# A two-layer hybrid encoder in split fp32: activation sums in program order, squares on VectorE, adding DMAs pinned

## The chip, the cores and the metric

The kernel runs on one core of a Trainium2 chip. Its time is the device time of one execution in microseconds (us); three executions gave 2105.25 (median), 2104.72 and 2109.62. The engines are named as in the profile: PE is TensorE, DVE is VectorE, ACT is ScalarE, POOL is GpSimd, SP is SyncE. Each engine takes its instructions in order; semaphores tie the engines together.

## The reference, cut to what matters

The program is a stack of two layers on x of 512 tokens by 1024 features. `D_FF` is 2816, that is 22 tiles of 128.

```python
def rms_norm(x, g):
    y = x * lax.rsqrt(jnp.mean(x * x, axis=-1, keepdims=True) + EPS)
    return y * g
def swiglu(u, w_gate, w_up, w_down):
    return (jax.nn.silu(u @ w_gate) * (u @ w_up)) @ w_down
...
for i in range(DEPTH):
    x = x + 0.5 * swiglu(rms_norm(x, ffn1_norm[i]), ffn1_w_gate[i], ffn1_w_up[i], ffn1_w_down[i])
    z = rms_norm(x, mix_norm[i]) @ w_in[i]
    ...   # four mixers on column groups of z: y_na, y_swa, y_dil, y_mla
    y = jnp.concatenate([rms_norm(y_na, ...), rms_norm(y_swa, ...), rms_norm(y_dil, ...), rms_norm(y_mla, ...)], axis=-1)
    x = x + y @ w_out[i]
    x = x + 0.5 * swiglu(rms_norm(x, ffn2_norm[i]), ffn2_w_gate[i], ffn2_w_up[i], ffn2_w_down[i])
    gate = jax.nn.sigmoid(rms_norm(x, ple_norm[i]) @ ple_w_gate[i])
    x = x + gate * (p[i] @ ple_w_proj[i])
return rms_norm(x, final_norm)
```

## The kernel before

**Numbers.** Everything is float32, but PE multiplies in fp32r. Each operand is therefore split into a high part (a rounding copy on ACT) and a low part (the difference, on DVE), and a product is three matmuls: wh with x high, wh with x low, wl with x high (`mm3`, lines 303 to 305). `cut` (L236 on ACT, L237 on DVE) splits a weight piece into a tile wh and a tile wl, three of each. `feed` with `split` (L156 on ACT, L157 on DVE) splits one 128 x 512 tile x[m] of the activations, times its norm gain. x is held transposed, features on partitions, as eight tiles x[0] to x[7].

**Norms.** The division by the root mean square comes after the matmul. For it, each x[m] is squared (L318 on ACT) and added to `acc` (L319: on POOL for m = 1 to 6, on DVE for m = 7). `rstat` sums over partitions on PE (L330), scales on DVE (L333) and takes the power -0.5 on POOL (L334, tile rc). `rspread` spreads rc over the partitions by PE transposes (L341) and copies the result to rb on ACT (L348); the gate of a tile waits for rb.

**The feed-forward.** An FFN goes over 22 tiles f in two halves of 12 and 10. Each f needs a gate matrix and an up matrix product. The first two f are "direct": four pieces each, every piece 12 matmuls on 512 columns. From there f goes in pairs. The gate stays dense (four "d" pieces of 12 matmuls by 512 columns a pair), but the up matrices of the pair and the two halves of the tokens make a 2 x 2 block product, done by seven products instead of eight (`seven`; a "product" is 12 matmuls of 256 columns, L412). ORDER interleaves them, `"ssdssdssdsd"`, and S_STEPS names the seven: X1, Z1, X2, Y, X3, Z2, X4. These need sums of activations (`combos`, L383 to L394, tiles TC, four sets a norm, made once per FFN) and sums of weight blocks (tiles S, four buffers). After the first half, and again after the second, the down projection runs eight output tiles.

**Sums of weights.** They are made by DMA: SP loads one block into S (L254), then POOL issues a DMA that adds another block from DRAM onto it (L256). For the next pair `sums` makes s1 = a21 + a22 and s2 = a21 + a22 + a11, so s2 takes two adding DMAs, here called s2a and s2b, and s2b must wait until s2a has landed. `factors` makes s3 = a11 + a21, and adds a12 onto s2 (L271, here "the a12 add") once s2 has been cut for its first use. The sum s2 + a12 is then cut again; it is the weight of the product Z2, the sixth of the pair.

**What sets the order.** The generator `plan` gives the weight pieces in the order of use; `take` pops one and `prep` keeps two ahead in the FFN. SP and PE run in the order written. On DVE, ACT and POOL a scheduler chooses the order, except for instructions handed to `keep_in_program_order` (also through `hold`, while `held` is true: at the start of the program).

**Crossings.** A stage hands x to the next one by adding its output to x[m], splitting x[m], squaring it. This document calls the end of the mixer's output projection (L1004 adds to x[m]) with the start of the second FFN "mixer to FFN 2", and the end of layer 0 (`ple_out`) with the start of layer 1 "gate to FFN 1". Mixer to FFN 2 occurs once in each layer, gate to FFN 1 once.

Of the kernel before, what the change touches and what calls it, by code (L numbers as in the profile page):

```python
# [18 lines left out]
KC = 8  # L19
# [18 lines left out]
class Encoder:  # L38
# [121 lines left out]
    def plan(self):  # L160
        a = self.a
        full = ((0, 4, 128), (512, 4, 128))
        for l in range(self.depth):
            for w in range(2):
                gu = a["ffn_gu"][l, w]
                for half in range(2):
                    c0, c1 = CUT[half], CUT[half + 1]
                    for f in range(c0, c1, 2):
                        if f == 0:
                            for n, g in enumerate(self.direct(l == w == 0, gu)):  # L170
                                yield g
                                if n == (4 if l == w == 0 else 7):
                                    sums = self.sums(gu[2, 1], gu[3, 1])
                            continue
                        s = self.factors(gu[f, 1], gu[f + 1, 1], sums)
                        d = self.slices((gu[f, 0], full), (gu[f + 1, 0], full))
                        for n, c in enumerate(ORDER):
                            yield s if c == "s" else d
                            if n == 3 and f + 2 < FF:
                                sums = self.sums(gu[f + 2, 1], gu[f + 3, 1])  # L180
                    for m in range(KC):
                        dn = a["ffn_d"][l, w, m]
                        yield from self.each((dn[:, c0:c0 + 8], full), (dn[:, c0 + 8:c1], ((0, c1 - c0 - 8, 128),)))
                if w == 0:
                    for i in range(M_END):
                        if i == M_DQ0:
                            for j in range(2):
                                yield from self.each((a["w_up"][l, j], ((0, 2, 256), (512, 1, 256))))
                        yield from self.each((a["w_in"][l, i], full))
                    for i in range(8):  # L190
                        yield from self.each((a["w_out"][l, i], full))
            for m in range(KC):
                pl = a["ple"][l, m]
                yield from self.each((pl[:, 0:4], ((0, 4, 128),)), (pl[:, 4:10], ((0, 3, 128), (384, 3, 128))))

    def direct(self, opening, gu):
        full = ((0, 4, 128), (512, 4, 128))
# [48 lines left out]
    def sums(self, a, b):  # L246

        flat = lambda src, k: src[:, k:k + 4].rearrange("p k m -> p (k m)")
        a11, a12, a21, a22 = flat(a, 0), flat(a, 4), flat(b, 0), flat(b, 4)
        nc = self.nc  # L250

        def load(first, *more):
            t = self.own("S", [128, T], F32, 4)
            nc.sync.dma_start(t, first)  # L254
            for src in more:
                nc.gpsimd.dma_start(t, src, accum_op=ALU.add)  # L256
            return t

        s1 = load(a21, a22)
        s2 = load(a21, a22, a11)  # L260
        return s1, s2, lambda: load(a11, a21), a12

    def factors(self, a, b, sums):
        s1, s2, third, a12 = sums
        raw, half = self.load(a), self.raw()
        yield self.cut(raw[:, 0:512], 4)
        s3 = third()
        yield self.cut(s1, 4)
        self.nc.sync.dma_start(half[:, 0:512], b[:, 4:8].rearrange("p k m -> p (k m)"))
        yield self.cut(s2, 4)  # L270
        self.nc.gpsimd.dma_start(s2, a12, accum_op=ALU.add)  # L271
        yield self.cut(raw[:, 512:1024], 4)
        yield self.cut(s3, 4)
        yield self.cut(s2, 4)
        yield self.cut(half[:, 0:512], 4)
# [48 lines left out]
    def rstat(self, acc, n, more=None):  # L324
        nc = self.nc
        ss = self.small()
        parts = [acc] if more is None else [acc, more]
        for i, p in enumerate(parts):
            for t in range(4):
                nc.tensor.matmul(ss[:, t:t + 1], lhsT=p[:, t * 128:(t + 1) * 128], rhs=self.ones,  # L330
                                 start=i == t == 0, stop=i == len(parts) - 1 and t == 3, skip_group_check=True)
        rc = self.tile("rc", [128, 4], F32, 3)
        nc.vector.tensor_scalar(out=rc, in0=ss[:, 0:4], scalar1=1.0 / n, scalar2=EPS, op0=ALU.mult, op1=ALU.add)  # L333
        nc.gpsimd.tensor_tensor(out=rc, in0=rc, in1=self.nhalf, op=ALU.pow)  # L334
        return rc

    def spread(self, rc):
# [13 lines left out]
    def begin(self, l, off):  # L351
        self.norm = (l, off)
        self.nacc = self.acc()
        self.xn = []

    def feed(self, m, square=True):
        nc = self.nc
        l, off = self.norm
        t = self.act()
        if l < self.depth:  # L360
            self.split(t, self.x[m], self.g(l, off, m))
        else:
            if m < KC - 1:
                self.squared(m)
            else:
                self.last = self.tmp()
                nc.scalar.activation(self.last, self.x[m], AF.Square)
            square = False
            t = t[:, 0].bitcast(F32)
            nc.scalar.activation(t, self.x[m], AF.Copy, scale=self.g(l, 0, m))  # L370
        self.xn.append(t)
        if square:
            self.squared(m)

    def squared(self, m, eng=None):
        nc = self.nc
        self.square(self.nacc, self.x[m], m == 0, eng or (nc.vector if m == KC - 1 else nc.gpsimd))

    def combos(self, l, off, j):
        nc = self.nc  # L380
        xg = self.keep().bitcast(F32)
        for e in range(2):
            nc.scalar.activation(xg[:, e], self.x[2 * j + e], AF.Copy, scale=self.g(l, off, 2 * j + e))  # L383
        f = self.keep().bitcast(F32).rearrange("p e (h t) -> p (e h) t", h=2)
        q = xg.rearrange("p e (h t) -> p (e h) t", h=2)
        nc.vector.tensor_tensor(out=f[:, 0:2], in0=q[:, 0::3], in1=q[:, 1:2].to_broadcast([128, 2, HT]),
                                op=ALU.subtract)
        nc.vector.scalar_tensor_tensor(f[:, 2], f[:, 0], -1.0, q[:, 3], op0=ALU.mult, op1=ALU.subtract)
        nc.vector.scalar_tensor_tensor(f[:, 3], f[:, 2], -1.0, q[:, 2], op0=ALU.mult, op1=ALU.subtract)
        out = []  # L390
        for i in (0, 2):
            t = self.own("TC", [128, 2, T], F32R, 8).rearrange("p e (h t) -> p e h t", h=2)
            nc.scalar.activation(t[:, :, 0], f[:, i:i + 2], AF.Copy)
            nc.vector.tensor_tensor(out=t[:, :, 1], in0=f[:, i:i + 2], in1=t[:, :, 0].bitcast(F32), op=ALU.subtract)  # L394
            out.append(t)
        return out

    def right(self, name, xs, tn):
        out = []
# [57 lines left out]
    def opening(self, gp, up):  # L457
# [5 lines left out]
                self.mm3(ps, (w[0][:, k % 4:], w[1][:, k % 4:]), xs[k:k + 1], start=k == 0, stop=k == KC - 1)  # L463
        for m in range(KC):
            self.squared(m, self.nc.vector)
        self.held = False

    def ffn(self, l, w, nxt):
        nc, a = self.nc, self.a
        xs, acc, rb, rc = self.xn, self.nacc, None, None  # L470
        off = G_FFN2 if w else G_FFN1
        self.ahead = 2
        tn, held = [], []
        for half in range(2):
            nf = CUT[half + 1] - CUT[half]
            hs = [self.big() if f < 7 else self.keep() for f in range(nf)]
            for f in range(2 if half == 0 else 0):
                gp, up = self.dense(), self.small()
                if l == w == f == 0:
                    self.opening(gp, up)  # L480
# [3 lines left out]
                if rc is not None:  # L484
                    rb, rc = self.rspread(rc), None
                    for j, hj in enumerate(held):
                        self.gated(*hj, rb, hs[j])
                    held = []
                self.mm3(gp, self.take(), xs[4:], start=False)
                self.full(up, xs)  # L490
                if rb is None:
                    rc = self.rstat(acc, D)
                    held.append((gp, up))
                else:
                    self.gated(gp, up, rb, hs[f])
            if half == 0:
                tn = [self.combos(l, off, j) for j in range(4)]
            for f in range(0 if half else 2, nf, 2):
                u = self.keep().bitcast(F32)
                s = self.seven(xs, tn, u)  # L500
                gps, grs, nd = [None] * 2, [None] * 2, 0
                for c in ORDER:
                    if c == "d":
                        e, part = divmod(nd, 2)
                        nd += 1
                        if part == 0:
                            gps[e] = self.dense()
                            self.mm3(gps[e], self.take(), xs[0:4], stop=False)
                            continue
                        self.mm3(gps[e], self.take(), xs[4:8], start=False)  # L510
                        grs[e] = self.gate(gps[e], rb)
# [387 lines left out]
    def mix(self, l, nxt):  # L899
# [103 lines left out]
        def out(m):  # L1003
            nc.vector.tensor_tensor(self.x[m], self.x[m], self.ops[m], op=ALU.add)  # L1004
            self.feed(m)

        for m in range(4):
            if m % 2 == 0:
# [68 lines left out]
    def ple_out(self, m, gp, pp, rb):  # L1077
# [4 lines left out]
        nc.vector.scalar_tensor_tensor(gr, gr, 1.0, pp, op0=ALU.add, op1=ALU.mult)  # L1082
        nc.vector.scalar_tensor_tensor(self.x[m], gr, 0.5, self.x[m], op0=ALU.mult, op1=ALU.add)
        self.feed(m)

    def ple_in(self, l):
        nc, a = self.nc, self.a
# [178 lines left out]
```

## Time and profile before

| | |
|---|---|
| median of three runs (lowest, highest) | 2105.25 us (2104.72, 2109.62) |
| profiled execution | 2106.33 us, its span 2104.6 us |
| PE | busy 2061.2 us, 98% of the span |
| DVE, ACT, POOL | 65%, 52%, 19% |
| granted TensorE clock, mean | 0.996 |
| chain that ended last, by engine | PE 88%, DVE 5%, ACT 3%, DMA 1%, issue 1% |

The span runs from the first to the last instruction; the profiled execution's own time is 1.7 us longer. Times inside the span are counted from its start. An arrow, as in `ps<-act,wl`, reads output from inputs. `[0.87 <-DVE wl L237]` after a row means that the engine sat idle 0.87 us before it and that DVE's instruction of line 237 on tile wl ended that wait. A row of a DMA issued by POOL has the time that POOL spent on the issue; the data land later.

### The profile page before, as it was taken

Reading aid. Unit: us, or ns where it says so; the run is one execution under the profiler, and the core shown is the slowest. Engines: PE = TensorE matmul, PEld = TensorE weight load, DVE = VectorE, ACT = ScalarE, POOL = GpSimd, SP = SyncE. Lnnn points to the kernel's source line nnn. Section 1 sums busy time; section 2 is a strip of 40 time slices with the busy share of each in tenths; the row PEclk is TensorE's granted clock in tenths of the full one; section 3 lists DMA queues with packets and bytes.
Section 4 is the critical chain, followed back from the end, with each engine's and each line's share of the span. In section 5 each row is a group of like instructions: output and inputs, shape, how many; then the busy total and the mean of one; then the engine's idle time right before and its main releaser. Section 6 shows DMA issues by size and latency. Waiting matters only on the chain.

```text
span 2104.6 us, 30073 instructions
## 1 busy us (share of the span) xinstructions
PE 2061.2 (98%) x11028; PEld 1761.4 (84%) x11028; DVE 1365.0 (65%) x2282; ACT 1089.1 (52%) x2057; POOL 393.5 (19%) x391
## 2 busy tenths in 40 slices
PE   8999999999999999999999999999999999999998
PEld 6988988887877988988889889888878789889886
DVE  7654666777777654666766546667787766546655
ACT  6442444687865442444644324437777644334434
POOL 2200101043322200101121002011433321002011
PEclk9999999999999999999999999999999999999999
DMA  7764753323126754753367457433121267457432
GB/s 221 181 163 115 189 135 112 96 66 81 51 61 150 188 145 118 187 140 103 118 148 191 131 137 177 125 102 108 62 81 60 67 167 183 125 144 182 128 93 85
DMA packets 109604, 269.07 MB, mean 128 GB/s; under 512 B 12688, under 2 KB 16912, under 8 KB 109456
## 3 DMA queue, kind: packets, MB, share of 16 engines
q1 hardware_dynamic: 79232, 208.89, 31.3%
q0 software_dynamic: 30080, 58.21, 16.2%
q8 instruction: 86, 1.41, 0.3%
q14 instruction: 62, 0.51, 0.1%
q10 hardware_dynamic: 144, 0.05, 0.0%
HBM read 262.91 MB, written 2.10 MB: 126 GB/s over the span
## 4 chain that ended last, share of the span: by engine, by line
PE 88%; DVE 5%; ACT 3%; DMA 1%; issue 1%; POOL 0%; SPq 0%; DVEq 0%; ACTq 0%; POOLq 0%
PE s L412 16%; PE ps L304 15%; PE ps L303 15%; PE ps L305 15%; PE s L303 6%; PE s L304 6%; PE s L305 6%; PE ps L412 3%; PE pv L677 2%; PE s L661 2%; ACT tmp L547 1%; PE s L619 1%; PE s L620 1%; DVE PT L665 1%; PE s L330 1%
## 5 line engine op out<-in xcount | busy, mean ns | idle before, releaser
L236 ACT ACTIVATE wh<-raw 128x512 fp32r<-128x512 f32 (+2 forms) x668 | 408.2, 612 | 578.9 <-PE ps L304 254.9
L237 DVE TENSOR_TENSOR wl<-raw,wh 128x512 fp32r<-128x512 f32 (+2 forms) x594 | 415.4, 700 | 259.3 <-ACT wh L236 251.6
L256 POOL DMA_DIRECT2D S<-in_ffn_gu x160 | 139.5, 880 | 910.1 <-DMA S<-in_ffn_gu 536.1
L303 PE MATMUL ps<-big,wh 128*128 128x512 f32 x632 | 253.0, 400 | 0.4 <-ACT big L156 0.4
L305 PE MATMUL ps<-big,wl 128*128 128x512 f32 x632 | 247.8, 392 | 3.1 <-DVE wl L237 3.1
L304 PE MATMUL ps<-big,wh 128*128 128x512 f32 x632 | 248.1, 393 | 0.9 <-DVE big L157 0.9
L303 PE MATMUL ps<-act,wh 128*128 128x512 f32 x624 | 248.9, 399 | 0.0
L305 PE MATMUL ps<-act,wl 128*128 128x512 f32 x624 | 244.2, 391 | 3.1 <-DVE wl L237 3.1
L304 PE MATMUL ps<-act,wh 128*128 128x512 f32 x624 | 244.4, 392 | 0.6 <-DVE act L157 0.6
L412 PE MATMUL s<-TC,wh 128*128 128x256 f32 x1280 | 236.1, 282 | 0.7 <-ACT rb L348 0.7
L412 PEld LDWEIGHTS s<-TC,wh 128*128 128x128 f32 x1280 | 205.7, 189 | 10.3 <-ACT rb L348 0.9
L237 DVE TENSOR_TENSOR wl<-S,wh 128x512 fp32r<-128x512 f32 x160 | 110.8, 692 | 122.3 <-ACT wh L236 121.1
L412 PE MATMUL s<-TC,wl 128*128 128x256 f32 x640 | 181.4, 283 | 0.0
L236 ACT ACTIVATE wh<-S 128x512 fp32r<-128x512 f32 x160 | 101.2, 633 | 149.3 <-DMA S<-in_ffn_gu 61.3
L305 PEld LDWEIGHTS ps<-big,wl 128*128 128x128 f32 x632 | 118.9, 188 | 29.9 <-DVE wl L237 4.0
L305 PEld LDWEIGHTS ps<-act,wl 128*128 128x128 f32 x624 | 117.1, 188 | 29.4 <-DVE wl L237 4.0
L304 PEld LDWEIGHTS ps<-big,wh 128*128 128x128 f32 x632 | 119.5, 189 | 21.7 <-DVE big L157 1.9
L303 PEld LDWEIGHTS ps<-big,wh 128*128 128x128 f32 x632 | 119.4, 189 | 20.7 <-ACT big L156 0.8
L237 POOL TENSOR_TENSOR wl<-raw,wh 128x512 fp32r<-128x512 f32 (+1 forms) x74 | 95.9, 1296 | 217.4 <-ACT wh L236 208.6
L304 PEld LDWEIGHTS ps<-act,wh 128*128 128x128 f32 x624 | 117.6, 188 | 20.8 <-DVE act L157 1.3
L303 PEld LDWEIGHTS ps<-act,wh 128*128 128x128 f32 x624 | 117.5, 188 | 19.6
L319 POOL TENSOR_TENSOR acc<-acc,tmp 128x512 f32<-128x512 f32 x48 | 67.1, 1398 | 349.6 <-ACT tmp L318 349.6
(244 smaller groups left out, 4346.7 us busy)
## 6 DMA issues: line engine op xcount, KB each, us to landing
raw<-in_ffn_gu SPq DMA_DIRECT2D x134, 512.0 KB, 5.1
S<-in_ffn_gu POOLq DMA_DIRECT2D x200, 256.0 KB, 4.8
raw<-in_ffn_d SPq DMA_DIRECT2D x64, 512.0 KB, 3.5
S<-in_ffn_gu SPq DMA_DIRECT2D x120, 256.0 KB, 3.8
raw<-in_w_in SPq DMA_DIRECT2D x40, 512.0 KB, 3.6
raw<-in_ffn_gu SPq DMA_DIRECT2D x44, 256.0 KB, 3.8
raw<-in_ffn_d SPq DMA_DIRECT2D x32, 256.0 KB, 2.6
raw<-in_w_out SPq DMA_DIRECT2D x16, 512.0 KB, 3.5
```

The lines of the kernel that those rows point to most:

```text
L236: self.hold(nc.scalar.activation(hi, r, AF.Copy))
L237: self.hold(self.side().tensor_tensor(out=lo, in0=r, in1=hi.bitcast(F32), op=ALU.subtract))
L256: nc.gpsimd.dma_start(t, src, accum_op=ALU.add)
L303: nc.tensor.matmul(ps, lhsT=wh[:, k], rhs=x[:, 0], start=start and k == 0, stop=False)
L304: nc.tensor.matmul(ps, lhsT=wh[:, k], rhs=x[:, 1], start=False, stop=False)
L305: nc.tensor.matmul(ps, lhsT=wl[:, k], rhs=x[:, 0], start=False, stop=stop and k == last)
L319: self.hold(eng.tensor_tensor(out=acc, in0=acc, in1=sq, op=ALU.add))
L330: nc.tensor.matmul(ss[:, t:t + 1], lhsT=p[:, t * 128:(t + 1) * 128], rhs=self.ones, start=i == t == 0, stop=i == len(parts) - 1 and t == 3 ...
L412: nc.tensor.matmul(ps, lhsT=v[:, k], rhs=x[:, e], start=start and k == i == 0, stop=k == 3 and i == 2, skip_group_check=True)
L547: nc.scalar.activation(sw[32 * b:32 * b + 32], p[32 * o:32 * o + 32], AF.Copy)
L661: nc.tensor.transpose(tp[:, t * 128:(t + 1) * 128], h["P"][t][:, o:o + 128], self.ident)
L677: nc.tensor.matmul(pv[:, c], lhsT=vb, rhs=h["pt"][b][:, i, c], start=b == 0 and i == 0, stop=b == 3 and i == 1, skip_group_check=True)
```

## The change

Line numbers after the change are larger: L237 becomes L241, L256 becomes L260, L271 becomes L275, L319 becomes L323, L334 becomes L338, L386 becomes L404, L1004 becomes L1032.

- **Sums of activations.** `combos` becomes a generator of two steps a set, and all its instructions are kept in program order. `some` issues one step at a time: at the entry of an FFN after x[4] and after x[5], the other steps between the direct pieces.
- **Splits.** While sums are due, the splits of x[6] and x[7] are kept in program order too.
- **Direct tiles.** The very first FFN takes four direct f instead of two, so it has one pair less; its spread of the norm moves behind the first dense piece of f = 2.
- **Squares.** All additions of squares go to VectorE.
- **POOL.** The power and all adding DMAs are kept in program order.

```diff
@@ plan
-                        if f == 0:
-                            for n, g in enumerate(self.direct(l == w == 0, gu)):
+                        if f < self.plainly(l, w):
+                            for n, g in enumerate(self.direct(l == w == f == 0, gu[f:f + 2])):
                                 yield g
-                                if n == (4 if l == w == 0 else 7):
-                                    sums = self.sums(gu[2, 1], gu[3, 1])
+                                if n == 7 and f + 2 == self.plainly(l, w):
+                                    sums = self.sums(gu[f + 2, 1], gu[f + 3, 1])
...
+    def plainly(self, l, w):
+        return 4 if l == w == 0 else 2
@@ sums, factors, rstat
-                nc.gpsimd.dma_start(t, src, accum_op=ALU.add)
+                self.tc.keep_in_program_order(nc.gpsimd.dma_start(t, src, accum_op=ALU.add))
...
-        self.nc.gpsimd.dma_start(s2, a12, accum_op=ALU.add)
+        self.tc.keep_in_program_order(self.nc.gpsimd.dma_start(s2, a12, accum_op=ALU.add))
...
-        nc.gpsimd.tensor_tensor(out=rc, in0=rc, in1=self.nhalf, op=ALU.pow)
+        self.tc.keep_in_program_order(nc.gpsimd.tensor_tensor(out=rc, in0=rc, in1=self.nhalf, op=ALU.pow))
@@ begin, feed, squared
+        self.tn, self.sums_due = [], []
+        if l < self.depth and off in (G_FFN1, G_FFN2):
+            self.sums_due = [g for g in [self.combos(l, off, j) for j in range(4)] for _ in range(2)]
+
+    def some(self, room=True):
+        if room and self.sums_due:
+            t = next(self.sums_due.pop(0))
+            if t:
+                self.tn.append(t)
...
+            held, self.held = self.held, self.held or m > 5 and bool(self.sums_due)
             self.split(t, self.x[m], self.g(l, off, m))
+            self.held = held
...
-        self.square(self.nacc, self.x[m], m == 0, eng or (nc.vector if m == KC - 1 else nc.gpsimd))
+        self.square(self.nacc, self.x[m], m == 0, eng or nc.vector)
@@ combos: every instruction goes through pin = self.tc.keep_in_program_order
...
+        yield
         out = []
...
-        return out
+        yield out
@@ ffn
-            for f in range(2 if half == 0 else 0):
+            nd0 = 0 if half else self.plainly(l, w)
+            for f in range(nd0):
...
+                self.some(f > 0)
                 self.mm3(gp, self.take(), xs[4:], start=False)
-                self.full(up, xs)
+                self.some()
+                xu = xs if f < 2 else xs[0::2] + xs[1::2]
+                self.mm3(up, self.take(), xu[0:4], stop=False)
+                self.some()
+                self.mm3(up, self.take(), xu[4:8], start=False)
...
+                self.some()
-            if half == 0:
-                tn = [self.combos(l, off, j) for j in range(4)]
-            for f in range(0 if half else 2, nf, 2):
+            self.held = False
+            for f in range(nd0, nf, 2):
...
                             self.mm3(gps[e], self.take(), xs[0:4], stop=False)
+                            if rc is not None:
+                                rb, rc = self.rspread(rc), None
+                                for j, hj in enumerate(held):
+                                    self.gated(*hj, rb, hs[j])
                             continue
@@ out (mixer) and ple_out
             self.feed(m)
+            self.some(m in (4, 5))
```

**Where instructions move.** First POOL in the steady part of an FFN, one pair. A number behind S names the buffer's tile: here S121 is the s3 of a pair, S97 that pair's s2, S135 and S136 the next pair's s1 and s2. Before:

```order
L256 DMA S121_611<-in_ffn_gu 128x512
L256 DMA S135_679<-in_ffn_gu 128x512
L256 DMA S136_682<-in_ffn_gu 128x512
L271 DMA S97_458<-in_ffn_gu 128x512
L256 DMA S136_682<-in_ffn_gu 128x512
```

After, with S149, S125, S163 and S164 in these places, and S188 the s3 that follows ("x2" are s2a and s2b, one behind the other):

```order
L260 DMA S149_767<-in_ffn_gu 128x512
L260 DMA S163_835<-in_ffn_gu 128x512
L260 DMA S164_838<-in_ffn_gu 128x512 x2
L275 DMA S125_614<-in_ffn_gu 128x512
L260 DMA S188_991<-in_ffn_gu 128x512
```

The a12 add (L271, now L275) stood between s2a and s2b of the next pair, and now stands behind s2b. s2b waits for the landing of s2a, as before.

Second DVE, mixer to FFN 2 of layer 0, from the addition to x[6] to the split of x[7]. L386, L388 and L394 (now L404, L406 and L413) belong to `combos`, L157 is the split, and wl the cut of a weight. Before:

```order
L1004 TENSOR_TENSOR x6_81<-x6_81,ps1336_6276 128x512
L237 TENSOR_TENSOR wl1344_6304<-raw1342_6301,wh1343_6303 128x512
L394 TENSOR_TENSOR TC1403_6544<-keep1402_6540,TC1403_6544 128x2x256
L157 SCALAR_TENSOR_TENSOR act1334_6270<-x5_80,gain_73,act1334_6270 128x512
L1004 TENSOR_TENSOR x7_82<-x7_82,s1341_6300 128x512
L386 TENSOR_TENSOR keep1406_6553<-keep1405_6550 128x512
L237 TENSOR_TENSOR wl1362_6341<-raw1342_6301,wh1361_6340 128x512
L394 TENSOR_TENSOR TC1404_6547<-keep1402_6540,TC1404_6547 128x2x256
L157 SCALAR_TENSOR_TENSOR act1339_6294<-x6_81,gain_73,act1339_6294 128x512
L388 SCALAR_TENSOR_TENSOR keep1406_6553<-keep1406_6553,keep1405_6550 128x256
L237 TENSOR_TENSOR wl1365_6347<-raw1363_6344,wh1364_6346 128x512
L157 SCALAR_TENSOR_TENSOR act1345_6320<-x7_82,gain_73,act1345_6320 128x512
```

After:

```order
L406 SCALAR_TENSOR_TENSOR keep1320_6185<-keep1320_6185,keep1319_6182 128x256
L323 TENSOR_TENSOR acc1301_6097<-acc1301_6097,tmp1326_6212 128x512
L241 TENSOR_TENSOR wl1355_6286<-raw1335_6246,wh1354_6285 128x512
L413 TENSOR_TENSOR TC1327_6215<-keep1320_6185,TC1327_6215 128x2x256
L1032 TENSOR_TENSOR x7_82<-x7_82,s1334_6245 128x512
L157 SCALAR_TENSOR_TENSOR act1332_6239<-x6_81,gain_73,act1332_6239 128x512
L407 SCALAR_TENSOR_TENSOR keep1320_6185<-keep1320_6185,keep1319_6182 128x256
L323 TENSOR_TENSOR acc1301_6097<-acc1301_6097,tmp1333_6242 128x512
L241 TENSOR_TENSOR wl1358_6292<-raw1356_6289,wh1357_6291 128x512
L241 TENSOR_TENSOR wl1360_6308<-raw1356_6289,wh1359_6307 128x512
L404 TENSOR_TENSOR keep1362_6326<-keep1361_6323 128x512
L157 SCALAR_TENSOR_TENSOR act1338_6265<-x7_82,gain_73,act1338_6265 128x512
```

The part of the first `combos` set that follows x[7]'s addition is gone from before the split, and additions of squares (L323) have come in. From the addition to x[4] to the split of x[7] DVE has 24 instructions before and 23 after (21 of 512 columns and 2 of 256).

Third POOL where layer 0 hands over to layer 1's first FFN. S2135 and S2136 are s1 and s2 of its first pair, S2141 is the s3, rc2123 the statistic of the norm. Before:

```order
L256 DMA S2135_10351<-in_ffn_gu 128x512
L256 DMA S2136_10354<-in_ffn_gu 128x512
L319 TENSOR_TENSOR acc1988_9720<-acc1988_9720,tmp2082_10144 128x512
L256 DMA S2141_10377<-in_ffn_gu 128x512
L256 DMA S2136_10354<-in_ffn_gu 128x512
L256 DMA S2171_10497<-in_ffn_gu 128x512
L334 TENSOR_TENSOR rc2123_10297<-rc2123_10297,nhalf_107 128x4
L256 DMA S2172_10500<-in_ffn_gu 128x512
L271 DMA S2136_10354<-in_ffn_gu 128x512
```

After, with S2138, S2139 and S2146 in these places, rc2120 the statistic of this norm, and rc1989 that of the gate's norm before it:

```order
L338 TENSOR_TENSOR rc1989_9706<-rc1989_9706,nhalf_107 128x4
L338 TENSOR_TENSOR rc2120_10255<-rc2120_10255,nhalf_107 128x4
L260 DMA S2138_10329<-in_ffn_gu 128x512
L260 DMA S2139_10332<-in_ffn_gu 128x512 x2
L260 DMA S2146_10361<-in_ffn_gu 128x512
L260 DMA S2160_10429<-in_ffn_gu 128x512
L260 DMA S2161_10432<-in_ffn_gu 128x512 x2
L275 DMA S2139_10332<-in_ffn_gu 128x512
```

The power stood behind five adding DMAs; now all adding DMAs of this FFN stand behind the power, and the addition of squares is gone from POOL.

## Rows read from the trace of the kernel before

**Rows 1.** The page: busy us, share of the span and instructions of each engine.

```profile
PE 2061.2 (98%) x11028; PEld 1761.4 (84%) x11028; DVE 1365.0 (65%) x2282; ACT 1089.1 (52%) x2057; POOL 393.5 (19%) x391
```

**Rows 2.** Waits of PE, 629 to 647 us: us in total, times, longest us.

```profile
PE ps L305 <- DVE wl L237: 3.5, 3, 2.3
PE s L305 <- DVE wl L237: 1.2, 1, 1.2
```

**Rows 3.** Windows: length; PE, PEld, DVE, ACT, POOL busy; granted clock; DMA share, GB/s.

```profile
629.00:647.00 18.00, 12.63 (x51) 8.65 (x49) 18.00 (x25) 12.62 (x23) 7.98 (x7) 1.00 0.49 129
1670.00:1688.00 18.00, 12.59 (x50) 8.69 (x49) 18.00 (x25) 12.62 (x23) 8.05 (x7) 1.00 0.50 128
1055.00:1069.00 14.00, 11.20 (x52) 8.49 (x51) 7.57 (x14) 5.50 (x9) 3.91 (x4) 1.00 0.66 145
1069.30:1072.60 3.30, 3.30 (x11) 2.62 (x10) 1.38 (x2) 1.23 (x2) 0.00 (x0) 0.50 0.07 11
330.00:378.00 48.00, 48.00 (x220) 39.85 (x219) 28.77 (x41) 19.22 (x34) 8.12 (x7) 1.00 0.36 109
```

**Rows 4.** Timeline of DVE, POOL there: start, us, instruction, idle before it.

```profile
639.80 2.88 DVE L386 TENSOR_TENSOR keep<-keep 128x512 f32<-128x512 f32 x1
638.96 1.87 POOL L256 DMA_DIRECT2D S<-in_ffn_gu  x2 [3.02 <-DVE TC L394]
640.19 1.93 POOL L319 TENSOR_TENSOR acc<-acc,tmp 128x512 f32<-128x512 f32 x1
```

**Rows 5.** Waits of PE, 1055 to 1069 us.

```profile
PE s L341 <- POOL rc L334: 2.1, 1, 2.1
```

**Rows 6.** Waits of PE, 12 to 37 us.

```profile
PE ps L304 <- DVE act L157: 2.0, 3, 1.1
PE s L412 <- ACT rb L348: 0.7, 1, 0.7
```

**Rows 7.** Timeline of PE: a product, a dense half, the next product.

```profile
99.40 0.40 PE L412 MATMUL s<-TC,wh 128*128 128x256 f32 x2
100.83 0.40 PE L303 MATMUL ps<-act,wh 128*128 128x512 f32 x1
103.58 0.40 PE L412 MATMUL s<-TC,wh 128*128 128x256 f32 x2
```

**Rows 8.** Timeline of POOL, ACT, DVE, PE: the pair at 98 us.

```profile
101.19 0.86 POOL L271 DMA_DIRECT2D S<-in_ffn_gu  x1 [0.47 <-DVE wl L237]
104.27 0.86 POOL L256 DMA_DIRECT2D S<-in_ffn_gu  x1 [2.22 <-DMA S<-in_ffn_gu]
108.08 0.63 ACT L236 ACTIVATE wh<-S 128x512 fp32r<-128x512 f32 x1 [2.03 <-DMA S<-in_ffn_gu]
108.75 0.69 DVE L237 TENSOR_TENSOR wl<-S,wh 128x512 fp32r<-128x512 f32 x1 [1.67 <-ACT wh L236]
110.87 0.28 PE L412 MATMUL s<-act,wl 128*128 128x256 f32 x1
```

**Rows 9.** Timeline of POOL, PE: the last typical pair, then a late one.

```profile
1925.63 0.86 POOL L256 DMA_DIRECT2D S<-in_ffn_gu  x1 [3.08 <-DMA S<-in_ffn_gu]
1931.19 0.28 PE L412 MATMUL s<-big,wl 128*128 128x256 f32 x1
230.50 0.86 POOL L256 DMA_DIRECT2D S<-in_ffn_gu  x1 [5.08 <-DMA S<-in_ffn_gu]
231.04 1.22 POOL L271 DMA_DIRECT2D S<-in_ffn_gu  x1
236.84 0.86 POOL L256 DMA_DIRECT2D S<-in_ffn_gu  x1 [4.58 <-DMA S<-in_ffn_gu]
239.43 0.39 PE L412 MATMUL s<-act,wl 128*128 128x256 f32 x1
```

**Rows 10.** Landing of the adds L271, and of the two at 638.96 and 639.62.

```profile
DMA to landing us min/median/max: 3.6/6.4/8.0
DMA to landing us min/median/max: 3.8/4.5/5.2
```

More of the change, by code (lines that the diff above doesn't have):

```diff
@@ L376, in squared @@
         nc = self.nc
-        self.square(self.nacc, self.x[m], m == 0, eng or (nc.vector if m == KC - 1 else nc.gpsimd))
+        self.square(self.nacc, self.x[m], m == 0, eng or nc.vector)
     def combos(self, l, off, j):
         nc = self.nc
+        pin = self.tc.keep_in_program_order
         xg = self.keep().bitcast(F32)
         for e in range(2):
-            nc.scalar.activation(xg[:, e], self.x[2 * j + e], AF.Copy, scale=self.g(l, off, 2 * j + e))
+            pin(nc.scalar.activation(xg[:, e], self.x[2 * j + e], AF.Copy, scale=self.g(l, off, 2 * j + e)))
         f = self.keep().bitcast(F32).rearrange("p e (h t) -> p (e h) t", h=2)
         q = xg.rearrange("p e (h t) -> p (e h) t", h=2)
[L386 to L389, printed above, removed]
+        pin(nc.vector.tensor_tensor(out=f[:, 0:2], in0=q[:, 0::3], in1=q[:, 1:2].to_broadcast([128, 2, HT]),
+                                    op=ALU.subtract))
+        pin(nc.vector.scalar_tensor_tensor(f[:, 2], f[:, 0], -1.0, q[:, 3], op0=ALU.mult, op1=ALU.subtract))
+        pin(nc.vector.scalar_tensor_tensor(f[:, 3], f[:, 2], -1.0, q[:, 2], op0=ALU.mult, op1=ALU.subtract))
+        yield
         out = []
@@ L392, in combos @@
             t = self.own("TC", [128, 2, T], F32R, 8).rearrange("p e (h t) -> p e h t", h=2)
-            nc.scalar.activation(t[:, :, 0], f[:, i:i + 2], AF.Copy)
-            nc.vector.tensor_tensor(out=t[:, :, 1], in0=f[:, i:i + 2], in1=t[:, :, 0].bitcast(F32), op=ALU.subtract)
+            pin(nc.scalar.activation(t[:, :, 0], f[:, i:i + 2], AF.Copy))
+            pin(nc.vector.tensor_tensor(out=t[:, :, 1], in0=f[:, i:i + 2], in1=t[:, :, 0].bitcast(F32),
+                                        op=ALU.subtract))
             out.append(t)
-        return out
+        yield out
     def right(self, name, xs, tn):
@@ L465, in opening @@
             self.squared(m, self.nc.vector)
-        self.held = False
     def ffn(self, l, w, nxt):
@@ L470, in ffn @@
         xs, acc, rb, rc = self.xn, self.nacc, None, None
-        off = G_FFN2 if w else G_FFN1
         self.ahead = 2
-        tn, held = [], []
+        held, tn = [], self.tn
         for half in range(2):
@@ L1084, in ple_out @@
         self.feed(m)
+        self.some(m in (4, 5))
     def ple_in(self, l):
```

## The prediction

> **What bounds the kernel now.** I read the page first: PE is busy 98% of the span [rows 1], so at most some 43 us are idle time, and anything that gains must take PE work away or one of PE's waits. The waits of PE over stretches come next. At the crossing from the mixer to FFN 2 PE waits for DVE's part of the cut weights, 3.5 and 1.2 us in layer 0 [rows 2]; the windows there show why: DVE is busy 18.00 of 18.00 us in layer 0 and again in layer 1, and PE 12.63 and 12.59, so 5.37 and 5.41 us are idle [rows 3]. At the gate to FFN 1 crossing 14.00 - 11.20 = 2.80 us are idle [rows 3], 2.1 of them in one wait for the power on POOL [rows 5], and just behind it a stretch of 3.30 us has PE busy at a granted clock of 0.50, the 1.2 GHz level, so half of it, 1.65, is lost [rows 3]. In the opening PE waits 2.0 for splits and 0.7 for rb [rows 6]. In the steady pairs PE hardly waits, but there I read the timeline, because the diff touches the order of POOL's adding DMAs: how late the sum for Z2 is, is what decides.
>
> **The opening and the direct tiles.** `combos` now comes behind the splits, and the norm is spread later; I take both waits as gone, 2.7. In the first FFN one pair of seven products becomes four dense pieces more. A product takes 100.83 - 99.40 = 1.43 and a dense piece 103.58 - 100.83 = 2.75 [rows 7]: 4 x 2.75 - 7 x 1.43 = 11.00 - 10.01 = +1.0. Sum -1.7; bounds +1.0 (nothing comes back) and -1.7.
>
> **The squares.** 48 additions leave POOL and join DVE. A whole DVE operation of this size took 0.69 [rows 8], so 33 us of DVE work. Most of it falls into projections such as the stretch from 330 to 378, where DVE is busy 28.77 of 48.00 and PE 48.00 [rows 3]: six additions, some 4 us, find 19 us free. I take nothing. At the crossings it is not free, and there it belongs to the next term. What it gives: DVE's L386 took 2.88 at 639.80, while POOL's L319 ran from 640.19 for 1.93 [rows 4]; the whole operation in rows 8 took 0.69, so 2.19 of that one is stretching beside POOL, which the change removes.
>
> **Mixer to FFN 2, twice.** In 18.00 us DVE does 25 operations, 0.72 each; without that one's stretching 15.81 / 25 = 0.63. From x[4]'s addition to x[7]'s split DVE had 24 operations, 24 x 0.72 = 17.3; now it has 21 whole and 2 half, 22 x 0.63 = 13.9. DVE ends the piece 3.4 sooner, and PE, which waited for it, gains that: 2 x 3.4 = 6.8 of 10.8. Some 2 us a crossing stay. Bounds: 0 and 10.8.
>
> **Gate to FFN 1, once.** The sums due are spread between direct pieces, so the 2.80 - 2.1 = 0.7 before go; the power no longer stands behind adding DMAs, so its 2.1 goes, and with it the slow clock, 1.65. Sum -4.5; bounds 0 and -4.5. In return the first pair's adding DMAs queue on POOL behind the power. That is covered: the power is needed after the first piece of f = 1, then three pieces of 2.75 and a product of 1.43 pass, 9.7 us, before the first sum is used, against a landing of some 4 to 5 us and 1.4 for the cut. I take nothing.
>
> So without POOL's new order: -1.7 - 6.8 - 4.5 = -13.0.
>
> **The a12 add behind s2b, in every pair.** Before, it is issued at 101.19 and s2b at 104.27, after idling 2.22 for the landing of s2a [rows 8]. Now the a12 add stands behind this wait. Two issues in a row stand 231.04 - 230.50 = 0.54 apart [rows 9], so it is issued at 104.81. If it lands F later, ACT's cut follows (0.67 until DVE starts, 108.75 - 108.08), then DVE's (0.69), and PE wants this wl at 110.87 [rows 8]: stall = 104.81 + F + 1.36 - 110.87 = F - 4.70. In the last pair, 1925.63 + 0.54 + F + 1.36 - 1931.19 = F - 3.66 [rows 9]. The 32 pairs of this kind lie around these; I take F - 4.1. What waits behind the a12 add on POOL is only the s3 add, needed much later; but ACT's and DVE's cuts for the piece after it wait too, so the stall is PE's own. It comes in each pair anew, since the next pair's adds follow cuts that PE's progress sets free.
>
> Three pairs have s2b later. There it comes at 236.84 and PE wants the weight at 239.43 [rows 9]: F - 0.69. But s2a took so long there because the a12 add ran beside it; of two issued together at 638.96 the first landed after 3.8 [rows 10], which would put s2b some 2.2 sooner. I take F - 2.9 for the three.
>
> What is F? The trace has no a12 add in this place. The adds L271 themselves landed after 3.6 at best, 6.4 in the middle, 8.0 at worst [rows 10], most of them with an add ahead and another issued behind. The nearest row is the pair of adds issued together at 638.96 [rows 4] with nothing issued for 5 us behind them: the second landed after 5.2 [rows 10]. That is the new a12 add's position, and I take 5.2. Then 32 x 1.1 + 3 x 2.3 = 35.2 + 6.9 = +42. At 3.6 the typical pairs cost nothing and the three late ones 3 x 0.7 = 2; at 6.4 it is 32 x 2.3 + 3 x 3.5 = +84. With this many pairs each 0.1 of F is 3.5 us.
>
> The Trainium skill, "DMA: Bandwidth & Descriptors", section on the anatomy of one DMA on the SWDGE (gpsimd) path, fits such a transfer as 2.0 us plus its bytes over 436e3 per us, an estimate of 2.6 us for these 256 KB. By that no pair stalls, and the sum would stay near -13 us; no adding DMA of the trace landed that soon, 3.6 being the least [rows 10], so the trace disagrees for these transfers.
>
> **The sum.** -13.0 + 42.1 = +29.1. The profiled execution took 2106.33, so 2135.4 in its terms; the median of the runs is 1.08 lower: 2134.
>
> **The rivals.**
>
> A, on the other side: the a12 add finds the queue almost empty and lands like a lone one, in 3.6 to 4.2. For it: in before it shared the queue with s2a ahead and s2b behind, and now only with s2b. Against it: the second add of the pair at 638.96 had only one neighbour too, and took 5.2. Then the pairs cost about 2, and the sum is -13.0 + 2 = -11: 2094. It decides below F = 4.37, where the cost equals the gains; within 0.3% (about 6.3 us, what a measurement here can tell from no change) it is between 4.19 and 4.55.
>
> B: F stays at the 6.4 of the line itself, because SP's loads for the next pair fall into the same 5 us. For it: that is the a12 add's own middle value. Against it: there it had adds on both sides. Then -13.0 + 84 = +71: 2176. Stalls above 2 us might then also bring the slow clock, as at 1069.
>
> C, the crossings don't get better: the additions of squares and the sums among the direct pieces keep DVE full. For it: four additions of squares now stand between x[4]'s addition and x[7]'s split. Against it: the counted 23 operations. Then the 6.8 is missing: 2141.
>
> D, adds as short as the fit above makes them: -13.0, 2092.
>
> **How the numbers follow.** The forecast, F between 4.6 and 5.9, gets 0.52; A 0.18; F between 4.2 and 4.6, 0.07; B 0.13; C 0.07; D 0.03. Faster by more than 0.3%: A, D and a little of what lies between, 0.22. Within 0.3%: 0.07. Slower: 0.71. The range takes in A, down to 2093, and B up to F = 6.3, 2172. The forecast alone goes from 2113 (F = 4.6) to 2159 (5.9).
>
> **What would show it.** In the profile after, the waits of PE should have a new line, `s` of the product for DVE's wl (or ACT's wh), some 35 times, about 1.1 each, at the third matmul or the first of Z2; in a pair the a12 add stands about 0.5 behind s2b; and its row of landings has a middle near 5.2. At the crossings the 5.4 should be about 2, the wait for the power gone, the clock at 1069 full. POOL has no L319. The prediction is wrong if the a12 add lands within 4.4, if it is issued sooner because s2a lands sooner, or if PE reaches Z2 later for another reason, so that the add is hidden after all.

## The result, and the profile after

| | before | after |
|---|---|---|
| median of the runs | 2106.16 us (4 runs, 2104.72 to 2109.62) | 2237.53 us (4 runs, 2217.76 to 2254.60) |
| ratio | | 1.0595, 95% interval 1.0560 to 1.0631 |
| span of the profiled execution | 2104.6 | 2215.5 |
| PE idle in the span, from the trace, us | 43.3 | 112.6 |
| PE busy at the lower clock (0.50), from the trace, us | 9.6 | 64.0 |

The ratio compares fast runs alone: the run of 2254.60 lies over 1.5% above the fastest of after and is left out of it, which leaves a median of 2231.57. By that the change makes the kernel slower by 125 us, and by 111 us between the two profiled executions; the one of after is the fastest of its four runs. The forecast was 2134, in a range from 2093 to 2172. The direction and the place were right, the size was not.

The page's row of busy time, after (compare [rows 1]): PE's busy time has risen by 42 us although the program has 36 matmuls fewer.

```profile
PE 2102.9 (95%) x10992; PEld 1786.6 (81%) x10992; DVE 1350.5 (61%) x2324; ACT 1074.9 (49%) x2050; POOL 325.0 (15%) x338
```

The waits of PE over the whole span, after (four lines of the view): what is waited for, us in total, times, longest. The first two are the waits at Z2 that were forecast; there was none before.

```profile
PE s L432 <- ACT wh L240: 75.8, 33, 6.0
PE s L432 <- DVE wl L241: 6.4, 29, 0.2
PE s L307 <- ACT wh L240: 2.9, 1, 2.9
PE s L309 <- DVE wl L241: 1.0, 1, 1.0
```

One pair after (POOL, ACT, PE), to be compared with [rows 8]. The a12 add (L275) stands 0.54 behind s2b, ACT's cut waits until it has landed, and PE waits at the first matmul of Z2 for wh and at the third for wl:

```profile
88.69 0.86 POOL L260 DMA_DIRECT2D S<-in_ffn_gu  x1 [3.03 <-DMA S<-in_ffn_gu]
89.23 1.22 POOL L275 DMA_DIRECT2D S<-in_ffn_gu  x1
95.49 0.63 ACT L240 ACTIVATE wh<-S 128x512 fp32r<-128x512 f32 x1 [5.47 <-DMA S<-in_ffn_gu]
94.49 0.29 PE L432 MATMUL s<-TC,wl 128*128 128x256 f32 x1
96.17 0.50 PE L432 MATMUL s<-act,wh 128*128 128x256 f32 x2 [1.40 <-ACT wh L240]
96.90 0.38 PE L432 MATMUL s<-act,wl 128*128 128x256 f32 x1 [0.22 <-DVE wl L241]
```

The rows also show a cost that is not counted as idle. In a running product a matmul of 256 columns follows the one before after 0.12 (12 in 1.43, [rows 7]). Here the one that follows 94.49 comes at 96.17, 1.68 later, and the one that follows the two from 96.17 at 96.90, where 0.24 would do: 1.56 + 0.49 = 2.05 us of delay, against 1.40 + 0.22 of idle time shown. The rest, 0.43 here, comes from the pipeline of PE, which runs empty and fills again: in the row of 94.49 a matmul takes 0.29, of which a running product hides all but 0.12 behind the next one, and a wait hides nothing.

Landing of the a12 add after, min, median and max (compare [rows 10]):

```profile
DMA to landing us min/median/max: 3.7/6.3/8.2
```

The second cost that was not forecast is the clock. Two stretches of after: length, busy time (instructions) of PE, PEld, DVE, ACT and POOL, granted clock, DMA share, GB/s. The first begins just behind a wait at Z2 of 4.1 us, the second 0.5 us before the end of one of 5.0. There are 17 stretches at the lower clock in the span, 82 us in all: 13 at waits at Z2, one at a wait in the opening, two in the mixers and one at the end. Before there were 3, with 18 us.

```profile
122.90:126.30 3.40, 3.40 (x13) 3.18 (x14) 3.40 (x7) 1.78 (x3) 0.00 (x0) 0.50 0.01 2
286.80:293.60 6.80, 6.29 (x20) 5.39 (x21) 5.57 (x10) 3.39 (x6) 0.00 (x0) 0.50 0.30 88
```

The crossings did get better. The waits of PE at the mixer to FFN 2 crossing of layer 0, 655 to 680 us, after (compare [rows 2]): 1.1 us in the place of 5.4, and layer 1 reads the same.

```profile
PE ps L308 <- DVE act L157: 0.7, 1, 0.7
PE ps L307 <- ACT act L156: 0.4, 1, 0.4
```

At the gate to FFN 1, 1100 to 1125 us (compare [rows 5]), the wait for the power is gone, with the slow stretch behind it:

```profile
PE ps L307 <- ACT big L156: 0.4, 1, 0.4
PE ps L308 <- DVE big L157: 0.3, 1, 0.3
```

**The account of the profiled executions**, from the intervals in which PE runs and the granted clock in them: waits at Z2 82.2; slow clock 27.2 (half of 64.0, less half of 9.6); pipeline filling 14.4 (what is left of the growth of PE's busy time, with the 1.0 that the direct tiles were forecast to cost); idle time elsewhere -12.9. The sum, 110.9, is the difference of the spans by construction. A count that does not rest on the remainder comes near it: from the starts of their matmuls the 35 pairs lose 98 us at Z2, 16 more than the idle time.

### The profile page after: what moved, and what is told of

It reads as the page before. It is cut to its first block, busy times and chain, and to the rows that moved or that the text cites. A ratio compares the mean times of both kernels' runs of the same rounds, so it can differ in the third digit from the quotient of the medians.

```text
span 2215.5 us, 29883 instructions
## 1 busy us (share of the span) xinstructions
PE 2102.9 (95%) x10992; PEld 1786.6 (81%) x10992; DVE 1350.5 (61%) x2324; ACT 1074.9 (49%) x2050; POOL 325.0 (15%) x338
## 5 line engine op out<-in xcount | busy, mean ns | idle before, releaser
L241 DVE TENSOR_TENSOR wl<-raw,wh 128x512 fp32r<-128x512 f32 (+2 forms) x595 | 395.1, 665 | 264.9 <-ACT wh L240 258.1
L260 POOL DMA_DIRECT2D S<-in_ffn_gu x156 | 136.7, 906 | 962.5 <-DMA S<-in_ffn_gu 695.3
L241 DVE TENSOR_TENSOR wl<-S,wh 128x512 fp32r<-128x512 f32 x156 | 107.9, 692 | 259.7 <-ACT wh L240 257.7
L307 PE MATMUL ps<-big,wh 128*128 128x512 f32 x632 | 255.1, 404 | 0.7 <-ACT big L156 0.7
L307 PE MATMUL ps<-act,wh 128*128 128x512 f32 x624 | 251.9, 404 | 0.4 <-ACT act L156 0.4
L309 PE MATMUL ps<-big,wl 128*128 128x512 f32 x632 | 249.1, 394 | 0.0
L309 PE MATMUL ps<-act,wl 128*128 128x512 f32 x624 | 245.8, 394 | 0.0
L432 PE MATMUL s<-TC,wh 128*128 128x256 f32 x1248 | 230.1, 282 | 0.0
L432 PEld LDWEIGHTS s<-TC,wh 128*128 128x128 f32 x1248 | 200.5, 189 | 9.1
L432 PE MATMUL s<-TC,wl 128*128 128x256 f32 x624 | 176.9, 284 | 0.0
L309 PEld LDWEIGHTS ps<-big,wl 128*128 128x128 f32 x632 | 120.0, 190 | 27.0 <-DVE wl L241 0.6
L309 PEld LDWEIGHTS ps<-act,wl 128*128 128x128 f32 x624 | 118.5, 190 | 26.5 <-DVE wl L241 0.3
L307 PEld LDWEIGHTS ps<-big,wh 128*128 128x128 f32 x632 | 121.1, 192 | 21.7 <-ACT big L156 1.6
L307 PEld LDWEIGHTS ps<-act,wh 128*128 128x128 f32 x624 | 119.3, 191 | 20.8 <-ACT act L156 0.8
L241 POOL TENSOR_TENSOR wl<-raw,wh 128x512 fp32r<-128x512 f32 (+1 forms) x74 | 95.6, 1291 | 217.2 <-ACT wh L240 211.9
L432 PEld LDWEIGHTS s<-TC,wl 128*128 128x128 f32 x624 | 117.7, 189 | 0.0
```

Of the source, the lines that this page charges most:

```text
L241: self.hold(self.side().tensor_tensor(out=lo, in0=r, in1=hi.bitcast(F32), op=ALU.subtract))
L260: self.tc.keep_in_program_order(nc.gpsimd.dma_start(t, src, accum_op=ALU.add))
L307: nc.tensor.matmul(ps, lhsT=wh[:, k], rhs=x[:, 0], start=start and k == 0, stop=False)
L309: nc.tensor.matmul(ps, lhsT=wl[:, k], rhs=x[:, 0], start=False, stop=stop and k == last)
L432: nc.tensor.matmul(ps, lhsT=v[:, k], rhs=x[:, e], start=start and k == i == 0, stop=k == 3 and i == 2, skip_group_check=True)
```

## The experiments

Theory 1: the loss is the place of the a12 add behind s2b's wait. Rival 1: other parts of the change cost too. Ratios are to the kernel before, run on the same chip in the same rounds; a time without a ratio is a median.

**The change without POOL's pinned adds.**

```diff
-                self.tc.keep_in_program_order(nc.gpsimd.dma_start(t, src, accum_op=ALU.add))
+                nc.gpsimd.dma_start(t, src, accum_op=ALU.add)
...
-        self.tc.keep_in_program_order(self.nc.gpsimd.dma_start(s2, a12, accum_op=ALU.add))
+        self.nc.gpsimd.dma_start(s2, a12, accum_op=ALU.add)
```

> The changed kernel, with the adding DMAs (L260, L275) no longer kept in program order; everything else stays. The a12 add then stands between s2a and s2b again. Theory 1 (the whole loss comes from the a12 add's place behind s2b's wait: 82 us of stalls at Z2, some 14 of refilling PE's pipeline, 27 of slow clock): no wait of PE for a weight at L432, three or fewer slow stretches, and a time of 2106 - 13 = 2093, between 2088 and 2098. Rival 1 (other parts cost too: squares and sums on DVE, the first pair's adds behind the power): 2110 to 2150, with waits for DVE or ACT elsewhere.

Measured 2108.72, ratio 1.0012 (1.0002 to 1.0021). The a12 add is back between s2a and s2b, and 80 of the 82 us at Z2 are gone. But the forecast of 2093 is missed by 16, and 2108.72 is below rival 1's range too. The waits of PE show a part of why:

```profile
PE s L345 <- POOL rc L338: 5.3, 3, 2.2
PE s L432 <- ACT wh L240: 1.7, 2, 0.9
```

The power now waits behind adding DMAs at three FFN starts, in the place of one before, and two of these waits are followed by a stretch of 3.4 us at the lower clock. The 5.3 of waiting and half of the two stretches make 8.7 of the 16; the rest was not traced. So the pins do two things: they cost 35 pairs a stall, and they keep the power ahead of the adds.

**The kernel before with the adds pinned, nothing else.** The same two lines, put into the kernel before the other way round.

> The kernel before, with nothing changed but the adding DMAs kept in program order, so that the a12 add comes behind s2b. Theory 1: it loses all that the change lost and the 13 us that the rest gave back: 2106 + 82 + 14 + 27 = 2230, between 2205 and 2255, with 30 or more waits at L412 and 10 or more slow stretches. Rival 1 (the other parts cost too): clearly less, 2130 to 2190.

Measured 2252.69, ratio 1.0686 (1.0639 to 1.0733): the pins alone lose all of it, and more than the change as a whole does. PE waits at L412:

```profile
PE s L412 <- ACT wh L236: 93.5, 33, 5.9
```

Theory 1 (2205 to 2255) holds with its sign and its size; rival 1 (2130 to 2190) is out as an account of the loss.

**s2b cut to 8 columns.** It leaves out the rest of the addition of a11.

```diff
-            for src in more:
-                self.tc.keep_in_program_order(nc.gpsimd.dma_start(t, src, accum_op=ALU.add))
+            for i, src in enumerate(more):
+                c = 8 if i else T
+                self.tc.keep_in_program_order(nc.gpsimd.dma_start(t[:, :c], src[:, :c], accum_op=ALU.add))
```

> The changed kernel with s2b cut down to 8 of its 512 columns (so s2 lacks the rest of a11), at its place and with its wait; the a12 add comes 0.5 us behind it as before. Theory 1 with the queue shared (the a12 add takes 6.4 us because s2b's 256 KB go through the same queue at once): it lands in 3.6 to 4.4, pairs with a slack of 5 us or more have no stall, some late pairs keep 1 to 3 us, time 2095 to 2120. Rival 2 (6.4 us is the a12 add's own, from loads of SP or a fixed cost): the landing stays at 6 to 6.5, the time at 2220 to 2240.

Measured 2162.52, ratio 1.0279 (1.0251 to 1.0308), between the two forecasts, so the time missed both; the landing is the theory's. Landing of the a12 add, and PE's waits at Z2:

```profile
DMA to landing us min/median/max: 3.6/4.3/6.7
```

```profile
PE s L433 <- ACT wh L240: 31.8, 17, 3.5
PE s L433 <- DVE wl L241: 4.3, 19, 0.2
```

So 2.0 of the 6.3 us are shared with s2b's 256 KB. What is left has its own share in the loss: even at 4.3 the late pairs stall. Between the a12 add and the moment PE is ready for Z2 (the end of the last matmul ahead of it) the traces have 9.5 us before (mean of 36 pairs), 5.1 after and 5.0 here; a landing of 4.3 and the two cuts (1.36, [rows 8]) do not fit in the eight pairs that leave only 1.6 to 4.1. These eight have 24 of the 36 us of waits; the rest falls in pairs whose a12 add lands later than 4.3, up to 6.7.

**The same pins, the sums begun one piece later.**

```diff
-                            if n == 3 and f + 2 < FF:
+                            if n == 4 and f + 2 < FF:
```

> The changed kernel, pins kept, but the next pair's sums are begun one weight piece later (after the fifth piece of a pair instead of the fourth), so that program order itself has the a12 add ahead of the next pair's s1 and s2. Theory 1: no stall at Z2, 2088 to 2098 like the kernel without pins, with the a12 add landing in 3.7 to 5. Rival 3 (order is not enough; the later start of s1 or s2 brings another wait, at Z1 or X2 of the next pair): 2100 to 2140 and waits at L432 in front of other products.

Measured 2094.38, ratio 0.9949 (0.9936 to 0.9961), as theory 1 had it. The a12 add is now written ahead of the next pair's sums, so the pins keep it there; POOL in one pair:

```profile
103.71 0.86 POOL L275 DMA_DIRECT2D S<-in_ffn_gu  x1 [9.42 <-DVE wl L241]
104.25 2.11 POOL L260 DMA_DIRECT2D S<-in_ffn_gu  x2
```

No wait at L432 is left, and the a12 add lands soonest of all, with no add just ahead of it:

```profile
DMA to landing us min/median/max: 3.6/3.8/6.2
```

**Matmuls in the wait.** A loop ahead of Z2 in the changed kernel, with a tile of zeros (`self.zero`, 128 x 256) set once. It runs in all 39 pairs, also in the four without a wait:

```diff
+            if name == "Z2":
+                for _ in range(20):
+                    self.nc.tensor.matmul(ps, lhsT=self.zero[:, 0:128], rhs=self.zero, start=False, stop=False,
+                                          skip_group_check=True)
```

> The changed kernel with 20 more matmuls of 256 columns by a zero tile, added into the bank of Z2 right before Z2 in every pair: about 20 x 0.12 = 2.4 us of PE work in the place of the wait, 35 x 2.4 = 84 us in all. Theory (the slow clock comes from PE's waits of about 3 us): waits up to 2.4 vanish, the longer ones keep some 22 us in sum, there are 0 to 6 slow stretches inside the pairs in the place of 14, and the time falls to 2195 to 2215 although PE does more. Rival (the slow clock comes from something else, or the wait is not what counts): 12 or more slow stretches, 2225 to 2260.

Measured 2242.34, ratio 1.0634 (1.0608 to 1.0660): the theory's time is missed, and it is the rival's (2225 to 2260). The waits fell as expected:

```profile
PE s L434 <- ACT wh L242: 28.3, 20, 3.5
PE s L434 <- DVE wl L243: 4.0, 18, 0.2
```

The slow stretches fell from 17 to 12, those at Z2 from 13 to 7, and the cost of all of them from 32 to 20 us. But PE's busy time apart from the clock grew by 87 us, which is more than the 50 us of waits and the 12 us of clock that went. In after, each of the ten waits at Z2 of 3 us and more has a slow stretch that begins in it or within 2 us behind it; but slow stretches also follow waits of 1.3 to 1.5 us (at 1336, 1987 and 2012), and with filling those of 1.9 to 2.0 us, while in after the waits of 2.5 and 2.4 us that end at 782 and 2039 have none. In these traces the clock falls at waits of PE, apart from the stretch at the end, and the length of a wait alone does not decide it. That the waits are the cause is argued from this; the time of this run does not show it.

**Squares back on POOL**, in the kernel with the sums one piece later:

```diff
-        self.square(self.nacc, self.x[m], m == 0, eng or nc.vector)
+        self.square(self.nacc, self.x[m], m == 0, eng or (nc.vector if m == KC - 1 else nc.gpsimd))
```

> The kernel with the sums one piece later (pins kept), with the squares of x[1] to x[6] back on POOL. Theory 2 (taking them off POOL is what repaired the crossings, since POOL's additions stretch DVE's): 3 to 7 us more than that kernel, 2097 to 2102, with waits of 2 to 4 us at each mixer to FFN 2 crossing and stretched DVE rows beside L323 on POOL. Rival 4 (the order of the sums repaired them, the squares do not matter): within 1.5 us of 2094.

Measured 2100.04, ratio 0.9967 (0.9955 to 0.9978). The interval overlaps that of the kernel it is compared with, which ran on another chip, so the question is put again below. PE's waits at the mixer crossing of layer 0:

```profile
PE ps L308 <- DVE act L157: 0.9, 2, 0.6
PE ps L307 <- ACT act L156: 0.6, 1, 0.6
PE ps L309 <- DVE wl L241: 0.2, 1, 0.2
```

1.7 us, where 5.4 was before and 1.1 without POOL's squares. So most of the repair comes from the rest of the change and not from the squares. POOL's order alone is the next run; the order of the sums of activations and of the splits was not run by itself.

**The kernel before, POOL in order.** All of POOL's adds and powers pinned, sums one piece later, nothing else of the change.

> The kernel before with POOL's adding DMAs and powers kept in program order and the next pair's sums begun one piece later, nothing else of the change. Theory 2: the wait for the power and the slow clock at the gate to FFN 1 go (2.1 and 1.65), the crossings stay as they were: 2105.3 - 3.8 = 2101.5, between 2099 and 2104. Rival 5 (POOL's order carries most of the gain, the crossings' waits only move): 2094 to 2097.

Measured 2099.41, ratio 0.9963 (0.9951 to 0.9976), in the theory's range. The wait for the power at the gate to FFN 1 and the slow stretch there are gone, as expected. The interval overlaps that of the kernel with the whole change and the sums one piece later (0.9936 to 0.9961), so POOL's order with the later sums carries most of that kernel's gain. The crossing did not stay as it was; it has lost a third of its waits, 3.6 us are left:

```profile
PE ps L305 <- DVE wl L237: 1.8, 3, 0.9
PE s L305 <- DVE wl L237: 1.2, 1, 1.2
PE ps L304 <- DVE act L157: 0.6, 1, 0.6
```

**Held cuts end early**, in the kernel with the sums one piece later:

```diff
         for m in range(KC):
             self.squared(m, self.nc.vector)
+        self.held = False
```

> The kernel with the sums one piece later, with the weight cuts of the first FFN's direct tiles no longer kept in program order (held ends after the first tile as in the kernel before). In that kernel PE waits 2.9 and 1.0 us near 40 us for cuts that stand behind sums and gated tiles, and the clock falls. Theory (the pinned cuts are the cause): both waits go, with the slow clock some 4 to 6 us, 2088 to 2091. Rival (the tiles' gated chain is the cause): same time, 2093 to 2095.5, the wait moves.

Measured 2087.72, ratio 0.9911 (0.9898 to 0.9925), and with the next two kernels again:

> The same kernel as e10_hold_ends_early, on the chip of the next two, so that they can be compared with it: 2086 to 2090.

Measured 2087.82, ratio 0.9916 (0.9902 to 0.9929). The waits for wh and wl at L307 and L309 near 40 us (2.9 and 1.0) are gone with the slow stretch behind them: they came from weight cuts pinned behind sums. This is the fastest version, 18 us below the kernel before. Its row of busy time:

```profile
PE 2058.4 (99%) x10992; PEld 1760.4 (84%) x10992; DVE 1357.5 (65%) x2324; ACT 1086.7 (52%) x2050; POOL 326.0 (16%) x338
```

**Two direct tiles**, in that kernel (`plainly` returns 2; sums still due are issued behind the tiles).

> e10 with two direct tiles in the first FFN, as in the kernel before (the sums that then find no place are issued in one go behind them). Theory (two tiles more cost four dense pieces for seven products, 1.0 us, and take away the waits of 2.7 at the opening, so they gain): 1 to 4 us more than e10, 2088 to 2092, with waits for rb or for sums between 30 and 50 us. Rival (the opening's waits had gone with the order of splits and sums): 1 us less than e10.

Measured 2098.99, ratio 0.9969 (0.9956 to 0.9981): 11 us more than with four, not 1 to 4. PE waits for sums of activations there, and the clock falls for 10.2 us:

```profile
PE s L432 <- ACT TC L412: 3.2, 1, 3.2
PE s L432 <- DVE TC L413: 2.8, 2, 1.8
```

```profile
36.30:46.50 10.20, 5.88 (x15) 4.52 (x16) 6.75 (x12) 4.33 (x9) 0.86 (x1) 0.50 0.70 138
```

**Squares on POOL in that kernel.**

> e10 with the squares of x[1] to x[6] back on POOL. From the earlier pair of kernels, where the crossings idled 1.9 us with them on POOL and 1.1 without: twice 0.8, and some tenths more in the opening, 1.5 to 4 us more than e10. Rival (no difference): within 1 us of e10.

Measured 2091.28, ratio 0.9932 (0.9920 to 0.9945): 3.5 us more than the same kernel without them on the same chip, as expected; the slowest run without them took 2089.59, the fastest with them 2090.65.

## Why the prediction was wrong

**The step that failed** is "I take 5.2" for F, the time until the a12 add lands. It is 6.3 in the middle and 6.4 in the mean of the 35 pairs. The other factor was nearly right: F - 4.1 for 32 pairs and F - 2.9 for three, with the cuts' 1.36, mean that on average 5.3 us pass from the issue to the end of the last matmul ahead of Z2; measured 5.1. So the idle time at Z2 became 82 us in the place of 42; 1.2 us more for F in 35 pairs are 42 us by the prediction's own sum. I had preferred the pair at 638.96 to the line's own median of 6.4 [rows 10], since that pair had nothing behind it. The line's own value was the better guess, and it was my rival B.

**Two costs were left out.** A stall was priced as idle time alone. The refilling of PE's pipeline, some 0.4 a pair, comes on top, 14 us; and the slow clock, 27 us, which I named for rival B only as something that "might" come, though before showed one after a wait of 2.1 us [rows 3, 5]. Rival B, with F = 6.4, came to 2176; these two, some 42 us, are the distance to the 2218 of the profiled run.

**Late pairs.** The mean was nearly right by luck, for its parts were not: I counted three late pairs. In after, eight have less than 4.6 us between the issue and PE's readiness. The first of each FFN but the first is among them, with 1.1, 0.05 and 1.2 us: its a12 add stands behind the next pair's s2b, and all of these adds stand behind the power. That was in the order, and I priced only what the first pair's own sums lost by the power. POOL and PE there:

```profile
699.81 1.22 POOL L275 DMA_DIRECT2D S<-in_ffn_gu  x1
700.59 0.29 PE L432 MATMUL s<-TC,wl 128*128 128x256 f32 x1
706.22 0.80 PE L432 MATMUL s<-act,wh 128*128 128x256 f32 x2 [5.34 <-ACT wh L240]
```

**The gains.** Idle time elsewhere fell by 12.9 us. I had 13.0 with 1.65 of clock in it, and that the two agree is chance, for the parts are others: the crossings gave 4.3 each, not 3.4 (DVE's piece from x[4]'s addition to x[7]'s split in layer 0 took 18.2 before and 13.7 after, 4.5 less); the gate 2.2 and its clock; the opening lost its 2.7 and 1.5 more and got 2.9 + 1.0 instead, from pinned cuts that I had not looked at; the mixers and the end gave 1.9 for which I had no term. Taking the squares off POOL is worth 3.5 us in all, but only some 0.5 at a crossing, where I had read 2.19 from the stretched row in [rows 4].

**The fit** of the Trainium skill ("DMA: Bandwidth & Descriptors", section on the anatomy of one DMA on the SWDGE (gpsimd) path) gives 2.6 us for 256 KB, an estimate. It is as far off here as in the trace of before: the soonest of the a12 adds in after landed in 3.7.

**Open.** Why an add behind another took 5.2 at 639.62 and 6.3 in the pairs is not settled: the part that s2b takes is shown, the other 1.1 is not. The traces point at SP's loads, which rival B had named. Over the landing of the add at 639.62 before and of the a12 add at 89.23 after (GB/s last):

```profile
639.62:644.78 5.16, 2.91 (x13) 1.93 (x12) 5.16 (x6) 3.22 (x6) 2.50 (x3) 1.00 0.73 111
89.23:95.39 6.16, 5.54 (x36) 4.84 (x34) 1.11 (x2) 0.79 (x2) 1.22 (x2) 1.00 0.89 202
```

In after, too, the second of two adds issued together landed after 5.0 at 679 and at 1780, where SP loaded nothing; but one at 1122, beside almost no load, took 6.2. Among the pairs, the landing goes only loosely with the bytes loaded in its first 4 us (correlation 0.33), and no run took the loads away. The times of after vary more, too: its runs lie 37 us apart, those of before 5. The granted clock over the span was 0.981 in the shortest of them and 0.971 in the longest; an estimate from these two puts some 23 of the 37 us down to the clock, and the rest was not measured.

## What to carry to other kernels

A pin freezes the order in which the code is written, so before an instruction is pinned one has to see what stands ahead of it on its queue and for what that waits; here one number in the generator, a piece later, turned 125 us of loss into a gain of 11. Price a stall that comes in every round with all three of its parts, the idle time, the refilling of the pipeline and the clock behind it. For the time of a transfer in a new place take its own row first, and multiply the doubt by the number of rounds before the forecast is written.

## What the runs showed that I had not expected

Two adds issued 0.5 us apart: the second landed after 6.3 us, after 4.3 when the first had 8 columns, and after 3.8 when no add was ahead of it. PE's granted clock fell to 0.50, for 3.4 or 6.8 us, at each of the ten waits at Z2 of 3 us and more and at three of 1.3 to 1.5 us. Matmuls put in the place of the wait brought a part of the clock back but cost more than they gave.
